# Second-layer S5 tables of a two-layer hybrid decoder: rotation tables as products of two tables of eight, GpSimd's products first, TensorE's parts later

## The chip, the cores and the metric

One core of a Trainium2 chip runs the whole program: two decoder layers over 512 tokens of width 1024, batch 1, in float32. The metric is the time of one execution on the device, in microseconds. The kernel before takes 1332.07 us in the median of 3 runs (1332.04 to 1332.51). TensorE is called PE in the rows of the profile, VectorE DVE, ScalarE ACT, GpSimd POOL; SP is the queue that issues the DMAs.

## What is computed

Each layer normalises x, projects it with `w_in`, sends parts of the result through three mixers (sparse attention, an S5 state-space group, a Mamba-2 group), projects back with `w_out` and adds; then it does the same with an MLP, `relu(h @ w_up)**2 @ w_down`. The change lies in the S5 group. What that group computes, cut to what matters:

```
step = exp(log_step); mag = exp(lr * step)
ab_re = mag * cos(li * step); ab_im = mag * sin(li * step)      # 16 groups x 64 complex states
bb_re, bb_im = ...                                              # input matrix, scaled by the step
x[s] = ab * x[s-1] + bb @ u[s]                                  # complex, along the 512 tokens
y[s] = Re(c @ x[s]) + d * u[s]
out  = gelu(y) * sigmoid(gelu(y) @ glu_w + glu_b)
```

All of `ab`, `bb` and `c` depend on the parameters alone, so the kernel makes tables of them which do not need the tokens.

## The kernel before, in words

**S5 in blocks of eight tokens.** The 512 tokens are 64 blocks (`C5`) of 8 (`T5`). Inside a block the recurrence is a matrix; from block to block the state is turned by the angle of `ab` to the power 8 and shrunk by `m8`, the magnitude to the power 8. The turning is taken out of the recurrence: VectorE multiplies by COS and SIN, scans with real factors, and turns back. `s5_tables` makes for each layer: the matrix `bb`; for each quarter `q` of the 16 groups the products `BPp` (bb times powers of ab, three GpSimd instructions) with `b0`, which TensorE transposes (tile `s5B`) and ScalarE copies to `BPT`; for each half the tables `COS` and `SIN`, 8 groups by 64 blocks; for each quarter the products `CA` (c times powers of ab), from which TensorE makes `s5st` (8 short matmuls in the trace for 4 in the code), ScalarE copies it to `strip`, GpSimd adds the term of `d`, and 8 DMAs on SP's queue spread it over the matrix `M` that GpSimd has cleared.

**COS and SIN before.** `s5_small` keeps cos and sin of the angle of one block times 1, 2, 4, ... 32 (`self.rot`, six pairs). A table starts with 1 and 0 in its first column and is doubled six times: columns k to 2k-1 are the first k turned by the angle of k blocks, with six instructions of 8k elements per half, 72 instructions in a layer.

**Who makes the order.** The program is written as streams (generators) that yield a length of time; `merge` always goes on with the stream whose clock is lowest. The instructions so written get ascending priorities, and a planner orders every engine's queue by priority and by when its own cost model takes each instruction to be ready. Engines run their queues in order. The first layer's tables are written beside its mixers (`mixers`). The second layer's are the stream `prepare`, written beside the first layer's MLP (`mlp`, 256 steps of 1.3 of the clock, 6 matmuls each); it starts at clock 120, and its GpSimd instructions are held behind the copy `gate` (L1395), which waits for the MLP's row statistics. While `prepare` runs, the pace of tables is that of the first layer, 0.3. A third stream, `stage`, splits the second layer's `w_in` and `w_out` into two parts and stores them in DRAM, through SP's queue as well. `rope_tables` of the second layer is written at the end of `prepare`.

**Buffers.** Tiles from `tt` share 16 buffers (tag "t"), tiles from `g` 52 (tag "g"). The scratch tiles `pt` have two buffers. A tile waits until an earlier tile's last reader has let its buffer go. In the kernel before the tables of one layer that live to the end are 4 BPT, 4 COS and SIN, 4 CA and 4 M, which is 16; bb, BPp and strip come from the same 16.

**Weights.** `Slabs` brings the weights through SP's queue (L176, or L167 for staged ones); ScalarE makes `whi` and VectorE `wlo` (L192) of each slab of the MLP. TensorE multiplies in three passes (L458 to L460).

Of the kernel before, what the change touches and what calls it, by code (L numbers as in the profile page):

```python
# [10 lines left out]
F32 = mybir.dt.float32  # L11
# [3 lines left out]
ALU = mybir.AluOpType  # L15
# [3 lines left out]
P = 128  # L19
# [15 lines left out]
G5 = 16  # L35
# [185 lines left out]
class Net:  # L221
# [271 lines left out]
    def s5_small(self):  # L493

        nc = self.nc
        v = nc.vector if S5_ON_DVE else nc.gpsimd
        n = L * G5
        o = _cc["lre"][0]
        lre = self.cols[:, o:o + n]
        o = _cc["lim"][0]  # L500
        lim = self.cols[:, o:o + n]
        o = _rr["lstep"][0]
        lst = self.rows[:, o:o + n]
        sg = self.tab_("sg")
        keep = lambda k: self.cp.tile([P, n], F32, name=f"s5{k}")
        tmp = self.small(n)
# [33 lines left out]
        ta = self.g([P, n, 4], name="s5ta")  # L540
# [21 lines left out]
        v.tensor_tensor(m8, m8, m8, ALU.mult)  # L562
        v.tensor_tensor(m8, m8, m8, ALU.mult)
        self.m8 = m8
        self.rot = []
        v.tensor_scalar(s1, s1, sg, None, ALU.mult)
        cc, ss = c1, s1
        for k in range(8):
            c2, s2 = (keep(f"rc{k}"), keep(f"rs{k}")) if k >= 2 else (tmp(), tmp())
            self.stt(v, s2, cc, 2.0, ss, ALU.mult, ALU.mult)  # L570
            v.tensor_tensor(t0, cc, cc, ALU.mult)
            v.tensor_tensor(t1, ss, ss, ALU.mult)
            v.tensor_tensor(c2, t0, t1, ALU.subtract)
            cc, ss = c2, s2
            if k >= 2:
                self.rot.append((cc, ss))
        yield 4.0

    def load_s5(self, l):
# [8 lines left out]
    def s5_tables(self, l, t):  # L588
# [38 lines left out]
            v.tensor_tensor(t, bu(u2), bw(w2), ALU.mult)  # L627
            v.tensor_tensor(out, out, t, ALU.add)

        for q in range(4):  # L630
            v = eng(f"B{q}")
            gs = slice(4 * q, 4 * q + 4)
            b0 = self.s([P, 4, 1, 16], tag=f"s5b0{q}", bufs=1)
            outer(v, b0, bbr, X, bbi, Y, gs, 0, 1)
            BPp = self.tt([P, 4, 16, 8], name="BPp")
            outer(v, BPp.rearrange("p g h d -> p g d h"), bbr, X, bbi, Y, gs, 1, 9)

            p = self.ps(self.bank["sB"], name="s5B")
            for j in range(4):
                nc.tensor.transpose(p[:, j * P:(j + 1) * P], BPp[:, j].rearrange("p h d -> p (h d)"), self.ident)  # L640
            bpt = self.tt([P, 4, P], name="BPT")
            nc.scalar.activation(bpt.rearrange("p g n -> p (g n)"), p, AF.Copy)
            t["b0"].append(b0)
            t["BPT"].append(bpt)
            yield self.pace["tab"] * 5.0

        for hf in range(2):
            v = eng(f"R{hf}")
            gs = slice(l * G5 + 8 * hf, l * G5 + 8 * hf + 8)
            cos = self.tt([P, 8, C5], name="COS")  # L650
            sin = self.tt([P, 8, C5], name="SIN")
            v.memset(cos[:, :, 0:1], 1.0)
            v.memset(sin[:, :, 0:1], 0.0)
            k = 1
            for j in range(6):
                ck, sk = [t[:, gs].unsqueeze(2).to_broadcast([P, 8, k]) for t in self.rot[j]]
                tmp = lambda: pt()[:, :8 * k].rearrange("p (g k) -> p g k", g=8)
                for out, op, f0, f1 in ((cos, ALU.subtract, ck, sk), (sin, ALU.add, sk, ck)):
                    ta, tb = tmp(), tmp()
                    v.tensor_tensor(ta, cos[:, :, :k], f0, ALU.mult)  # L660
                    v.tensor_tensor(tb, sin[:, :, :k], f1, ALU.mult)  # L661
                    v.tensor_tensor(out[:, :, k:2 * k], ta, tb, op)
                k *= 2
            t["COS"].append(cos)
            t["SIN"].append(sin)
            yield self.pace["tab"] * 13.0
        pool.tensor_scalar(bc[1], bc[1], self.tab_("sg"), None, ALU.mult)
        for q in range(4):
            v = eng(f"C{q}")
            gs = slice(4 * q, 4 * q + 4)  # L670
            ca = self.tt([P, 4, 8, 16], name="CA")
            outer(v, ca, cre, X, cim, Y, gs, 0, 8)
            p = self.ps(self.bank["sst"], (16, 4, 8, 16), name="s5st")
            for j in range(4):
                nc.tensor.matmul(p[:, j].rearrange("p d h -> p (d h)"), t["b0"][q][:, j, 0], ca[:, j].rearrange("p d h -> p (d h)"),
                                 start=True, stop=True)
            strip = self.tt([16, 4, 8, 16], name="strip")
            nc.scalar.activation(strip, p, AF.Copy)

            sh = [16, 4, 16]  # L680
            d = pt()[:16, :64].rearrange("p (g h) -> p g h", g=4)
            pool.tensor_tensor(d, self.ident[:16, :16].unsqueeze(1).to_broadcast(sh), dd[:, gs].unsqueeze(2).to_broadcast(sh), ALU.mult)
            pool.tensor_tensor(strip[:, :, 0], strip[:, :, 0], d, ALU.add)
            m = self.tt([P, 4, P], name="M5")
            pool.memset(m, 0.0)
            for i in range(8):
                nc.sync.dma_start(m[7 - i::8, :, i * 16:], strip[:, :, 0:8 - i].rearrange("p g d h -> p g (d h)"))
            t["CA"].append(ca)
            t["M"].append(m)
            yield self.pace["tab"] * 5.0  # L690


    def s5(self, l, tab, U, out):
# [888 lines left out]
```

## Time and profile before

| | |
|---|---|
| Median of 3 runs | 1332.07 us |
| Profiled execution | 1328.87 us |
| Its span | 1327.1 us |
| TensorE busy | 1218.0 us, 92% |
| VectorE busy | 885.2 us, 67% |
| ScalarE busy | 549.2 us, 41% |
| GpSimd busy | 169.7 us, 13% |
| Chain that ended last | TensorE 62%, VectorE 19%, issue 7%, GpSimd 6%, ScalarE 4% |

The span is the time between the first and the last instruction of the profiled execution; its own time includes what lies around. Busy shares are means over stages with different limits: the first layer's mixers lie between 0 and about 330 us, its MLP from there to about 700, the second layer's mixers up to about 960, and its MLP behind them.

### The profile page before, as it was taken

The page shows a single profiled execution, that of the slowest core. Times are in us where ns is not written, and L with a number is a line of the kernel's source. Part 1 is how long each engine was busy: PE and PEld are TensorE (multiplying, and loading weights), DVE is VectorE, ACT ScalarE, POOL GpSimd, SP SyncE. Part 2 cuts the span into 40 slices and gives each one's busy share as a digit, 9 for nine tenths or more (in the row PEclk, how much of TensorE's full clock was granted, in tenths as well). Part 3 has the DMA queues.
Part 4 walks back from the last instruction along what each step waited for, and adds up shares of the span by engine and source line. Part 5 has one row for each costly group of instructions (what it writes and reads, how often), then busy time and mean ns, then how long its engine had stood idle before and what let it go on. Part 6 is the DMA issues. An engine that isn't in the chain of part 4 may idle for free.

```text
span 1327.1 us, 17056 instructions
## 1 busy us (share of the span) xinstructions
PE 1218.0 (92%) x5708; PEld 977.1 (74%) x5708; DVE 885.2 (67%) x2024; ACT 549.2 (41%) x1128; POOL 169.7 (13%) x302
## 2 busy tenths in 40 slices
PE   5678957889999989999999989968999999999998
PEld 5566745458888868888888767754788888888887
DVE  5998999857886545665564699975475445444443
ACT  4245444664543533534443234455254233242331
POOL 2385100000796040000000000000000000000000
PEclk9889988899999999999999989978999999999999
DMA  5132220002567647677644634300323333333332
GB/s 189 40 88 70 74 74 24 9 1 72 148 213 257 214 146 252 224 262 230 227 149 137 219 120 124 120 17 1 111 88 97 101 97 96 96 96 99 100 110 81
DMA packets 139688, 161.64 MB, mean 122 GB/s; under 512 B 18768, under 2 KB 107600, under 8 KB 139600
## 3 DMA queue, kind: packets, MB, share of 16 engines
q1 hardware_dynamic: 139600, 160.55, 38.5%
q8 instruction: 45, 0.74, 0.2%
q14 instruction: 43, 0.35, 0.1%
HBM read 128.29 MB, written 31.03 MB: 120 GB/s over the span
## 4 chain that ended last, share of the span: by engine, by line
PE 62%; DVE 19%; issue 7%; POOL 6%; ACT 4%; DMA 1%; SPq 0%; ACTq 0%; DVEq 0%; POOLq 0%
PE pm L458 18%; PE pm L460 18%; PE pm L459 18%; PE po L1128 3%; DVE isc L1087 2%; DVE mx L1086 2%; DVE isc L1076 2%; PE pTp L1123 1%; DVE pe L1107 1%; DVE wlo L192 1%; DMA wraw<-in_w_in_dram 1%; POOL pt L660 1%; DVE cv L847 1%; ACT pe L1108 1%; POOL pt L661 1%
## 5 line engine op out<-in xcount | busy, mean ns | idle before, releaser
L192 DVE TENSOR_TENSOR wlo<-wraw,whi 128x512 fp32r<-128x512 f32 (+1 forms) x312 | 223.2, 718 | 243.0 <-ACT whi L191 241.4
L191 ACT ACTIVATE whi<-wraw 128x512 fp32r<-128x512 f32 (+1 forms) x312 | 194.1, 625 | 374.5 <-PE pm L459 236.9
L458 PE MATMUL pm<-xh,whi 128*128 128x512 f32 x640 | 252.4, 395 | 3.8 <-ACT q L1224 3.2
L460 PE MATMUL pm<-xh,wlo 128*128 128x512 f32 x640 | 250.1, 392 | 1.2 <-DVE wlo L192 1.2
L459 PE MATMUL pm<-xl,whi 128*128 128x512 f32 x640 | 250.9, 392 | 0.0
L460 PE MATMUL pm<-uh,wlo 128*128 128x512 f32 x512 | 199.7, 390 | 0.3 <-DVE wlo L192 0.3
L458 PE MATMUL pm<-uh,whi 128*128 128x512 f32 x512 | 199.6, 390 | 0.0
L459 PE MATMUL pm<-ul,whi 128*128 128x512 f32 x512 | 199.6, 390 | 0.0
L458 PEld LDWEIGHTS pm<-xh,whi 128*128 128x128 f32 x640 | 120.8, 189 | 30.8 <-ACT q L1224 3.9
L460 PEld LDWEIGHTS pm<-xh,wlo 128*128 128x128 f32 x640 | 120.6, 189 | 27.4 <-DVE wlo L192 2.0
L459 PEld LDWEIGHTS pm<-xl,whi 128*128 128x128 f32 x640 | 121.1, 189 | 24.2 <-issue 0.2
L460 PEld LDWEIGHTS pm<-uh,wlo 128*128 128x128 f32 x512 | 96.2, 188 | 20.8 <-DVE wlo L192 0.9
L459 PEld LDWEIGHTS pm<-ul,whi 128*128 128x128 f32 x512 | 96.3, 188 | 20.4 <-issue 0.4
L458 PEld LDWEIGHTS pm<-uh,whi 128*128 128x128 f32 x512 | 96.2, 188 | 20.3 <-issue 0.4
L458 PE MATMUL pm<-whi,xh 128*128 128x512 f32 (+1 forms) x176 | 67.4, 385 | 14.0 <-ACT xh L392 12.8
L460 PE MATMUL pm<-whi,xl 128*128 128x512 f32 (+1 forms) x176 | 66.6, 380 | 1.3 <-DVE xl L394 1.3
L459 PE MATMUL pm<-wlo,xh 128*128 128x512 f32 (+1 forms) x176 | 67.0, 381 | 0.5 <-DVE wlo L192 0.3
L1408 DVE TENSOR_TENSOR ul<-ur,uh 128x512 fp32r<-128x512 f32 x64 | 48.5, 758 | 21.0 <-ACT uh L1407 21.0
L1406 DVE SCALAR_TENSOR_TENSOR ur<-pm,ur 128x512 f32<-128x512 f32 x64 | 43.9, 686 | 23.0 <-ACT ur L1403 22.7
L1414 DVE TENSOR_TENSOR sq<-pm,r2b 128x512 f32<-128x512 f32 x64 | 44.1, 689 | 17.5 <-PE pm L460 17.5
L1407 ACT ACTIVATE uh<-ur 128x512 fp32r<-128x512 f32 x64 | 39.9, 624 | 30.7 <-DVE ur L1406 30.7
L1087 DVE MATCH_REPLACE8 isc<-mx,isc 128x256 f32<-128x256 f32 (+2 forms) x96 | 51.6, 541 | 0.0
(345 smaller groups left out, 1931.4 us busy)
## 6 DMA issues: line engine op xcount, KB each, us to landing
wraw<-in_w_up_dram SPq DMA_DIRECT2D x128, 256.0 KB, 2.8
wraw<-in_w_down_dram SPq DMA_DIRECT2D x128, 256.0 KB, 2.8
st<-shi SPq DMA_DIRECT2D x48, 256.0 KB, 2.9
st<-slo SPq DMA_DIRECT2D x48, 256.0 KB, 3.5
wlo<-st SPq DMA_DIRECT2D x48, 256.0 KB, 3.0
whi<-st SPq DMA_DIRECT2D x48, 256.0 KB, 2.8
wraw<-in_w_in_dram SPq DMA_DIRECT2D x32, 256.0 KB, 2.8
sraw<-in_w_in_dram SPq DMA_DIRECT2D x32, 256.0 KB, 3.9
```

Of the source, the lines that this page charges most:

```text
L191: nc.scalar.activation(hi, raw, AF.Copy)
L192: nc.vector.tensor_tensor(lo, raw, hi.bitcast(F32), ALU.subtract)
L458: nc.tensor.matmul(p, lh, rh, start=first, stop=False)
L459: nc.tensor.matmul(p, lh, rl, start=False, stop=False)
L460: nc.tensor.matmul(p, ll, rh, start=False, stop=last)
L1076: v.scalar_tensor_tensor(acc, r, wi[:, h:h + 1], acc, ALU.mult, ALU.add)
L1087: v.match_replace(acc, m8, acc, SENT)
L1128: nc.tensor.matmul(po[g_ * 64:g_ * 64 + 64], self.vt[:, kb, g_], pts[g_], start=kb == 0, stop=kb == b)
L1406: v.scalar_tensor_tensor(r, p, 0.0, r, ALU.max, ALU.mult)
L1407: nc.scalar.activation(h, r, AF.Copy)
L1408: v.tensor_tensor(lo, r, h.bitcast(F32), ALU.subtract)
L1414: v.tensor_tensor(t, d[1], rb, ALU.mult)
```

## The change

`rotc` and `rots` hold the six kept pairs as one tile each, so that the pairs for 1, 2, 4 and those for 8, 16, 32 blocks can be taken together (`j::3`). `c8` and `s8` are two tables of eight for all 16 groups: the angle of 0 to 7 blocks, and that of 0, 8, ... 56 blocks. They are made by three doublings of 32, 64 and 128 elements, 18 instructions in a layer. `COS` and `SIN` are then the products of the two: three instructions of 512 elements for each of them and each half, 12 in a layer.

`powers` and `turned`, and `taps` and `kernels`, are the two loops over `q`, each cut in two: GpSimd's products, and what follows them on TensorE, ScalarE, GpSimd (the term of `d`, clearing M) and SP. In the first layer the halves stand together as before. In the second the products are all written first, then 90 of the clock pass, then come the four `turned` and the four `kernels`, 6 of the clock apart. `strip` moves from the 16 buffers of "t" to the 52 of "g". The rotation step's pace goes from 13.0 to 7.0.

```diff
@@ s5_small
-        self.rot = []
+        self.rotc, self.rots = [self.cp.tile([P, 6, n], F32, name=self.nm("rot")) for _ in range(2)]
...
-            c2, s2 = (keep(f"rc{k}"), keep(f"rs{k}")) if k >= 2 else (tmp(), tmp())
+            c2, s2 = (self.rotc[:, k - 2], self.rots[:, k - 2]) if k >= 2 else (tmp(), tmp())
...
@@ s5_tables
-        for q in range(4):
+        def powers(q):
             v = eng(f"B{q}")
...
+            return b0, BPp
+        def turned(b0, BPp):
             p = self.ps(self.bank["sB"], name="s5B")
...
+        todo = []
+        for q in range(4):
+            todo.append(powers(q))
+            if l == 0:
+                turned(*todo[q])
             yield self.pace["tab"] * 5.0
+        v = eng("R0")
+        gs = slice(l * G5, (l + 1) * G5)
+        c8, s8 = [self.tt([P, 2, G5, 8], name=n) for n in ("c8", "s8")]
+        v.memset(c8[:, :, :, 0:1], 1.0)
+        v.memset(s8[:, :, :, 0:1], 0.0)
+        k = 1
+        for j in range(3):
+            ck, sk = [t[:, j::3, gs].unsqueeze(3).to_broadcast([P, 2, G5, k]) for t in (self.rotc, self.rots)]
+            tmp = lambda: pt()[:, :2 * G5 * k].rearrange("p (i g k) -> p i g k", i=2, g=G5)
+            for out, op, f0, f1 in ((c8, ALU.subtract, ck, sk), (s8, ALU.add, sk, ck)):
+                ta, tb = tmp(), tmp()
+                v.tensor_tensor(ta, c8[:, :, :, :k], f0, ALU.mult)
+                v.tensor_tensor(tb, s8[:, :, :, :k], f1, ALU.mult)
+                v.tensor_tensor(out[:, :, :, k:2 * k], ta, tb, op)
+            k *= 2
...
+            lo = [t[:, 0, 8 * hf:8 * hf + 8].unsqueeze(2).to_broadcast(sh8) for t in (c8, s8)]
+            hi = [t[:, 1, 8 * hf:8 * hf + 8].unsqueeze(3).to_broadcast(sh8) for t in (c8, s8)]
+            for out, op, x, y in ((cos, ALU.subtract, lo[0], lo[1]), (sin, ALU.add, lo[1], lo[0])):
+                o = out.rearrange("p g (a b) -> p g a b", a=8)
+                t8 = pt().rearrange("p (g a b) -> p g a b", g=8, a=8)
+                v.tensor_tensor(o, hi[0], x, ALU.mult)
+                v.tensor_tensor(t8, hi[1], y, ALU.mult)
+                v.tensor_tensor(o, o, t8, op)
...
-            yield self.pace["tab"] * 13.0
+            yield self.pace["tab"] * 7.0
...
-            strip = self.tt([16, 4, 8, 16], name="strip")
+            strip = self.g([16, 4, 8, 16], name="strip")
...
+        for q in range(4):
+            taps(q)
+            if l == 0:
+                kernels(q)
             yield self.pace["tab"] * 5.0
+        if l > 0:
+            yield 90.0
+            for q in range(4):
+                turned(*todo[q])
+                yield 6.0
+            for q in range(4):
+                kernels(q)
+                yield 6.0
```

## Rows read from the trace of the kernel before

**Rows 1.** Windows by stage: length, busy (count) per engine, TensorE clock, DMA.
```profile
76.00:99.00 23.00, 20.80 (x97) 15.96 (x95) 22.83 (x47) 13.27 (x27) 21.12 (x42) 0.93 0.33 92
...
115.00:170.00 55.00, 49.87 (x253) 38.31 (x252) 54.81 (x166) 27.75 (x63) 14.41 (x21) 1.00 0.28 75
300.00:455.00 155.00, 155.00 (x706) 128.94 (x705) 115.35 (x167) 69.19 (x122) 77.41 (x124) 1.00 0.58 179
455.00:500.00 45.00, 39.84 (x186) 31.34 (x185) 22.26 (x32) 16.80 (x30) 15.00 (x28) 0.96 0.52 157
500.00:700.00 200.00, 199.70 (x894) 165.25 (x892) 117.92 (x185) 84.72 (x147) 0.31 (x1) 1.00 0.69 224
770.00:840.00 70.00, 60.78 (x315) 48.98 (x314) 69.77 (x202) 27.13 (x58) 0.53 (x1) 0.93 0.41 127
...
490.00:495.00 5.00, 5.00 (x21) 3.70 (x19) 0.69 (x1) 1.22 (x2) 1.97 (x5) 0.76 0.19 29
```

**Rows 2.** TensorE's waits, whole span: total us, times, longest us.
```profile
PE s5st L675 <- POOL CA L628: 6.8, 3, 3.7
...
PE s5B L640 <- POOL BPp L628: 4.9, 1, 4.9
```

**Rows 3.** TensorE's timeline: start us, duration us, instruction, [idle before, releaser].
```profile
482.58 1.05 PE L675 MATMUL s5st<-CA,s5b 128*16 128x128 f32 x8 [1.42 <-POOL CA L628]
...
489.42 1.89 PE L675 MATMUL s5st<-CA,s5b 128*16 128x128 f32 x8 [3.75 <-POOL CA L628]
...
492.80 0.40 PE L460 MATMUL pm<-uh,wlo 128*128 128x512 f32 x1
...
504.72 1.05 PE L675 MATMUL s5st<-CA,s5b 128*16 128x128 f32 x8
...
506.73 0.39 PE L459 MATMUL pm<-ul,whi 128*128 128x512 f32 x1
...
510.82 0.50 PE L460 MATMUL pm<-uh,wlo 128*128 128x512 f32 x1 [0.30 <-DVE wlo L192]
```

**Rows 4.** GpSimd's timeline, from the gate to the second layer's last M.
```profile
340.80 0.56 POOL L1395 COPY gate<-r 128x4 f32<-128x4 f32 x1 [170.60 <-DVE r L1390]
...
377.86 0.65 POOL L660 TENSOR_TENSOR pt<-COS,s5rc 128x8 f32<-128x8 f32 x1
...
416.75 0.74 POOL L662 TENSOR_TENSOR SIN<-pt,pt 128x256 f32<-128x256 f32 x1
...
460.44 1.06 POOL L626 TENSOR_TENSOR CA<-s5bc,s5X 128x512 f32<-128x512 f32 x1 [37.93 <-PE s5B L640]
...
488.11 1.25 POOL L628 TENSOR_TENSOR CA<-CA,pt 128x512 f32<-128x512 f32 x1
...
794.38 0.53 POOL L685 MEMSET M<- 128x512 f32 x1 [287.55 <-PE s5v L709]
```

**Rows 5.** GpSimd's groups: operation, out<-in, count | busy us, mean ns | idle before.
```profile
L628 POOL TENSOR_TENSOR CA<-CA,pt 128x512 f32<-128x512 f32 x7 | 9.3, 1323 | 0.2
...
L626 POOL TENSOR_TENSOR CA<-s5bc,s5X 128x512 f32<-128x512 f32 x7 | 7.7, 1107 | 44.0 <-PE s5B L640 37.9 <-PE s5v L709 4.7 <-DMA M<-strip 1.4
...
L662 POOL TENSOR_TENSOR COS<-pt,pt 128x128 f32<-128x128 f32 x4 | 2.6, 642 | 0.3
```

**Rows 6.** VectorE's instruction ul (L1408) in two windows: length, busy (count), clock, DMA.
```profile
341.00:377.00 36.00, 8.56 (x6) 1.00 0.60 173
...
520.00:680.00 160.00, 11.01 (x16) 1.00 0.72 233
```

**Rows 7.** SP's queue, timeline: start us, duration us, line, DMA, count.
```profile
100.54 38.49 SPq L176 DMA_DIRECT2D wraw<-in_w_in_dram  x10
...
147.69 5.13 SPq L687 DMA_DIRECT2D M<-strip  x8
...
481.46 16.91 SPq L687 DMA_DIRECT2D M<-strip  x24
...
499.62 0.38 SPq L176 DMA_DIRECT2D wraw<-in_w_down_dram  x1
```

More of the change, by code (lines that the diff above doesn't have):

```diff
@@ L574, in s5_small @@
             cc, ss = c2, s2
-            if k >= 2:
-                self.rot.append((cc, ss))
         yield 4.0
@@ L647, in s5_tables @@
         for hf in range(2):
             v = eng(f"R{hf}")
-            gs = slice(l * G5 + 8 * hf, l * G5 + 8 * hf + 8)
             cos = self.tt([P, 8, C5], name="COS")
             sin = self.tt([P, 8, C5], name="SIN")
[L652 to L663, printed above, removed]
+            sh8 = [P, 8, 8, 8]
@@ L664, in s5_tables, with taps @@
             t["COS"].append(cos)
             t["SIN"].append(sin)
-            yield self.pace["tab"] * 13.0
+            yield self.pace["tab"] * 7.0
         pool.tensor_scalar(bc[1], bc[1], self.tab_("sg"), None, ALU.mult)
-        for q in range(4):
+        def taps(q):
             v = eng(f"C{q}")
@@ L672, in s5_tables, with kernels @@
             outer(v, ca, cre, X, cim, Y, gs, 0, 8)
+            t["CA"].append(ca)
+        def kernels(q):
+            gs = slice(4 * q, 4 * q + 4)
+            ca = t["CA"][q]
             p = self.ps(self.bank["sst"], (16, 4, 8, 16), name="s5st")
@@ L687, in s5_tables @@
                 nc.sync.dma_start(m[7 - i::8, :, i * 16:], strip[:, :, 0:8 - i].rearrange("p g d h -> p g (d h)"))
-            t["CA"].append(ca)
             t["M"].append(m)
+        for q in range(4):
+            taps(q)
+            if l == 0:
+                kernels(q)
             yield self.pace["tab"] * 5.0
+        if l > 0:
[6 more added lines that the diff above has]
+                yield 6.0
     def s5(self, l, tab, U, out):
```

## The prediction

> **What bounds the kernel now.** I read the page first (TensorE is busy for nine tenths of the span), then the windows by stage, then TensorE's waits, then the timelines of TensorE, GpSimd and the SP queue around the one hole that the windows show.
>
> The windows tell two kinds of stage apart [rows 1]. In the first layer's mixers VectorE is the full engine: 22.83 of 23 us from 76 to 99, 54.81 of 55 us from 115 to 170. In the first layer's MLP TensorE is: 155.00 of 155 us from 300 to 455, 199.70 of 200 us from 500 to 700. Between these lies the hole: from 455 to 500 TensorE is busy for 39.84 of 45 us. Here the second layer's tables are made beside the MLP. A microsecond that TensorE loses in an MLP is lost to the end, since nothing else is waited for there; a microsecond saved on GpSimd is worth only what somebody waits for it.
>
> TensorE's waits name the cause [rows 2]: its matmuls s5st wait for GpSimd's product CA, 6.8 us in three waits. Two are the hole, 1.42 us at 482.58 and 3.75 us at 489.42 [rows 3], together 5.17; the other 1.6 us lie in the first layer. In the hole's second half the granted clock is 0.76 [rows 1].
>
> GpSimd's timeline says why CA is late [rows 4]. The gate opens at 340.80; GpSimd makes BPp, turns the rotation tables from 377.86 to 417.49, begins CA, and then stands for 37.93 us until 460.44, waiting for TensorE's transposes s5B. The pool "t" has 16 buffers, and the next CA needs one that a BPp holds. TensorE reaches s5B only where the written order puts it, at the planner's clock 120. After it, three quarters of CA are still to be made while TensorE is due to use them a few microseconds later; the CA of 488.11 (1.25 us) ends at 489.36, and s5st starts at 489.42.
>
> **The change part by part.**
>
> *Second layer, order.* All GpSimd products are written at clock 120 to 136 and need 1 (bb) + 4 (BPp) + 2 (c8, s8) + 4 (COS, SIN) + 4 (CA) = 15 buffers of "t", which is within 16 since the strip moves to "g". So GpSimd no longer waits for TensorE. From the gate: BPp until some 377 as today, then the rotations, then CA. One CA takes two products of about 1.11 us and a sum of 1.32 us [rows 5], 3.5 us; four take 14.2 us. Everything is made by about 420. TensorE's parts follow at clock 120 + 4 x 1.5 + 2 x 2.1 + 4 x 1.5 + 90 = 226.2, the matmuls s5st from 250.2 to 268.2. A step of the MLP is 6 matmuls and 1.3 of the clock; 894 matmuls in 200 us [rows 1] make it 1.34 us, so a unit of the clock is 1.03 us. With clock 120 at 460, the transposes come at about 570 and s5st at 594 to 613, 150 us and more behind the last product. Both waits go:
> - idle time, 1.42 + 3.75 = 5.17 us [rows 3];
> - the slow clock behind the second: from the start of s5st to the fifth of the MLP's matmuls behind it, 492.80 - 489.42 = 3.38 us, against 506.73 - 504.72 = 2.01 us for the same piece at full clock [rows 3]: 1.37 us.
>
> Sum: 6.54 us, all on the path. The matmuls themselves, their evictions and the strips are the same in number and only move.
>
> *The moved steps on SP's queue.* Each of the four kernel steps issues 8 DMAs of M. Today 24 of them take SP 16.91 us without a break [rows 7], 0.70 us each, so 5.6 us for a step, now one every 6.2 us for 25 us, past which the weight loads must squeeze. Today SP brings no weights between 481.46 and 499.62, and TensorE loses 0.30 us to weights at 510.82 [rows 3]; but it stood for 5.17 us in that time. Bounds: -0.30 us (that wait goes) and +5.5 us (SP falls behind as far as today, and the 5.17 us of standing, in which TensorE used no weights, come on top of the 0.30). I take 0, nearest to the 0.30 of the row: loads now get in between four bursts.
>
> *Rotation tables.* 72 instructions of 8 to 256 elements per layer, 39.6 us in the second [rows 4], become 18 of 32 to 128 elements and 12 of 512. The long ones cost 1.11 to 1.32 us [rows 5], 13.3 to 15.8 us; the short ones at most 0.64 us (the 128-element row), 11.5 us at most. So 25 to 27 us at most, at least 12 us off GpSimd in each layer. In the second layer this lies in front of that lead and is worth nothing more. In the first, SIN and COS are read by VectorE long behind GpSimd's end, and VectorE is full; I take 0. Bounds: -1.6 us (the first layer's wait of s5st for CA [rows 2] goes) and +4.9 us (the largest wait of TensorE for a GpSimd product, s5B for BPp [rows 2], appears once more because the planner puts s5st earlier).
>
> *Long GpSimd instructions beside VectorE.* Where GpSimd ran 512-element instructions (341 to 377), VectorE's subtraction ul took 8.56 / 6 = 1.43 us; with GpSimd silent it took 11.01 / 16 = 0.69 us [rows 6]. The first layer's 12 long instructions will run at about 85 to 100, where VectorE is full. Between nothing and 12 x 0.74 = 8.9 us, I take 0: fewer GpSimd instructions in all stand against longer ones, the CA products that followed move to an earlier, less crowded stretch, and ul is one kind of instruction among many there. The Trainium skill, SBUF — State Buffer, section "Who interferes with whom", says that a VectorE instruction with two SBUF inputs and a GpSimd instruction that reads SBUF exclude one another for a whole instruction, whichever starts first. The rows on ul agree in kind; taken at its word for all twelve, it gives the third rival below.
>
> *The last M.* It no longer waits for a buffer until the second layer's s5v (794.38, after 287.55 us [rows 4]), and 8 DMAs leave SP's queue there. VectorE is full at that place, 69.77 of 70 us [rows 1], so 0; bounds 0 and -5.6 us (a whole burst off the path).
>
> **Sum.** The profiled execution took 1328.87 us (span 1327.1, 1.8 us around it). Less 6.5 this is 1322.4. The median of the runs, 1332.07, is 3.2 us above that execution; on its scale the forecast is 1332.07 - 6.5 = **1325.6 us**.
>
> **Rivals.**
> 1. *The moved DMAs crowd out the MLP's weights.* Four bursts, 90% of SP's time over 25 us, staging stores between them. For it: SP runs in order, and a burst that waits for its strip holds the loads behind it. Against: SP was closed for 18 us in one piece and TensorE lost 0.30. Price 5.5 us, the upper bound above: 1331.1 us.
> 2. *The other side: the first layer's M overtakes the projection weights.* Today SP ends its W_in loads at 139.03 and begins M at 147.69 [rows 7]. The rotations end at least 12 us sooner there, and with them CA, s5st and M may move up to about 135, in front of the last W_in loads, which then stand behind bursts of 5.6 us in a stage whose VectorE is full. Two bursts cost 11.3 us: 1325.6 + 11.3 = 1336.9 us. It decides from two bursts issued before the last W_in load. Against it: the first layer keeps its written order (every part of TensorE right behind its product), and M also waits for s5st in TensorE's own order, which a quicker GpSimd alone does not move.
> 3. *Long GpSimd instructions hold VectorE*, at full price, in the first layer: 1325.6 + 8.9 = 1334.5 us. For it: [rows 6]. Against: as above.
> 4. *The change doesn't do what it says*: TensorE still meets an unfinished product, because the planner takes the moved parts early. Against: BPp is done when the rotations start (377.86 [rows 4]), and TensorE takes s5B only before 460, in its written place. It would leave 1332.1 us.
>
> **How the numbers follow.** Forecast 0.60 (its own range 1321 to 1328.5), rival 1 0.10, rival 2 0.15, rival 3 0.10, rival 4 0.05. About 0.2% (2.7 us) is what a measurement of this kernel tells from no change: below 1329.4 is faster, above 1334.7 slower. Faster: 0.58 of the forecast and 0.02 of rival 1, whose price is a bound, 0.60. Slower: 0.13 of rival 2 and 0.04 of rival 3, 0.17. The rest, 0.23, is no change. The range from 1320.5 to 1335.0 leaves out about 0.05 below (the bounds of the first layer and of the last M both paid) and 0.14 above (most of rival 2).
>
> **What would show it.** TensorE's waits from 300 to 700 without s5st behind CA; TensorE busy without a hole until the MLP's end, granted clock 1.00 throughout; GpSimd's products in one piece from the gate to about 420, with no wait for s5B; s5B near 570 and s5st near 594 to 613; the memset of the last M before the second layer. The MLP of the first layer should be 6.5 us shorter, and the second layer as long as before. The forecast is wrong if TensorE waits for weights between 590 and 625 (rival 1), if the first layer's mixers are longer, with loads behind M on SP before 140 (rival 2) or VectorE's single instructions grow longer from 76 to 115 (rival 3), or if the second layer's length changes by more than 2 us.

## The result and the profile after

The kernel after took 1355.81 us, the median of four runs (1352.55 to 1357.84), against 1332.29 us before (1332.04 to 1332.91) on the same chip: a ratio of 1.0173, 95% interval 1.0155 to 1.0191. It is 1.7% slower. The forecast was 1325.6 us, with a range up to 1335.0: wrong in sign, and outside its range.

The profiled execution took 1357.66 us (span 1355.9; before 1327.1). Two marks divide the 28.8 us between the two spans: the gate, at which the first layer's MLP begins, and the last `rst` of VectorE, a few us into the second layer. The two executions lie further apart than the medians do (28.8 against 23.5 us): that of before ran 3.4 us below its median, that of after 1.9 us above. So the marks say where the time is lost; how much is better read from the medians.

| us | before | after | difference |
|---|---|---|---|
| first layer's mixers, start to gate | 340.80 | 368.71 | +27.9 |
| first layer's MLP, gate to last `rst` | 378.03 | 378.88 | +0.85 |
| second layer, to the end of the span | 608.3 | 608.3 | 0 |

Windows of after: length, busy time (count) of TensorE, weight load, VectorE, ScalarE, GpSimd; clock, DMA, GB/s. The first, third, fifth and last answer to [rows 1], the latter two moved by 28 us.

```profile
76.00:99.00 23.00, 15.97 (x72) 12.06 (x71) 22.93 (x36) 11.38 (x25) 22.12 (x31) 0.87 0.25 69
84.00:116.00 32.00, 15.65 (x69) 11.64 (x67) 31.73 (x31) 10.99 (x23) 28.67 (x31) 0.82 0.16 46
115.00:170.00 55.00, 51.08 (x244) 38.71 (x244) 46.98 (x137) 28.62 (x64) 4.50 (x7) 0.94 0.28 72
185.00:300.00 115.00, 81.71 (x407) 60.50 (x406) 94.58 (x255) 54.55 (x142) 0.00 (x0) 0.80 0.09 26
483.00:528.00 45.00, 45.00 (x200) 37.26 (x199) 29.08 (x47) 19.00 (x33) 0.00 (x0) 1.00 0.77 251
650.00:680.00 30.00, 24.21 (x99) 18.94 (x98) 13.93 (x21) 13.04 (x23) 3.81 (x13) 0.94 0.78 242
798.00:868.00 70.00, 60.55 (x315) 48.74 (x314) 69.81 (x203) 26.49 (x56) 0.00 (x0) 0.93 0.40 123
```

From 84 to 116 VectorE is busy throughout, with 31 instructions; before it did 49 in 26.73 us of that window. From 185 to 300, in the later part of the mixers, TensorE does 407 matmuls at a granted clock of 0.80, before 468 at 0.88. From 483 to 528 the hole of [rows 1] is closed: TensorE 45.00 of 45 us. A new one lies from 650 to 680. TensorE's waits of after from 345 to 745 are a single row, where [rows 2] had CA, and its timeline shows both pieces:

```profile
PE pm L458 <- ACT whi L191: 5.8, 2, 4.7
```
```profile
652.06 0.50 PE L458 MATMUL pm<-xh,whi 128*128 128x512 f32 x1 [1.12 <-ACT whi L191]
...
668.18 0.80 PE L458 MATMUL pm<-xh,whi 128*128 128x512 f32 x1 [4.66 <-ACT whi L191]
```

GpSimd's timeline of after (start, duration), against [rows 4]: from the gate to the last sum of CA (450.54) it does not wait for TensorE, and the four memsets of M stand well ahead of the second layer.

```profile
368.71 0.56 POOL L1433 COPY gate<-r 128x4 f32<-128x4 f32 x1 [196.33 <-DVE r L1428]
...
450.54 1.28 POOL L627 TENSOR_TENSOR CA<-CA,pt 128x512 f32<-128x512 f32 x1
...
598.49 0.53 POOL L710 MEMSET M<- 128x512 f32 x1 [145.97 <-PE s5B L642]
...
618.98 0.53 POOL L710 MEMSET M<- 128x512 f32 x1 [5.41 <-PE s5B L642]
```

SP's timeline of after (start, duration, count), against [rows 7]: in the first layer two bursts of M stand ahead of the last loads of `w_in`; in the MLP SP brings no weights between 625.81 and 648.23.

```profile
139.40 5.54 SPq L712 DMA_DIRECT2D M<-strip  x8
146.00 3.74 SPq L176 DMA_DIRECT2D wraw<-in_w_in_dram  x3
153.94 5.02 SPq L712 DMA_DIRECT2D M<-strip  x8
159.06 0.53 SPq L176 DMA_DIRECT2D wraw<-in_w_in_dram  x1
...
625.81 0.38 SPq L176 DMA_DIRECT2D wraw<-in_w_up_dram  x1
...
627.76 5.02 SPq L712 DMA_DIRECT2D M<-strip  x8
...
635.75 5.00 SPq L712 DMA_DIRECT2D M<-strip  x8
...
643.11 5.01 SPq L712 DMA_DIRECT2D M<-strip  x8
648.23 1.04 SPq L176 DMA_DIRECT2D wraw<-in_w_up_dram  x2
...
654.27 5.47 SPq L712 DMA_DIRECT2D M<-strip  x8
```

What VectorE does so long from 84 to 116 is read from two timelines of after side by side, VectorE's first, then GpSimd's.

```profile
93.39 1.08 DVE L1040 TENSOR_TENSOR rsw<-qi,cols 128x64 f32<-128x64 f32 x1
94.40 1.08 DVE L1033 TENSOR_TENSOR ksb<-ksb,rsw 128x48 f32<-128x48 f32 x1
95.41 1.33 DVE L1041 TENSOR_TENSOR rsw<-qi,cols 128x64 f32<-128x64 f32 x1
96.77 1.06 DVE L1042 TENSOR_TENSOR qi<-qi,cols 128x128 f32<-128x128 f32 x1
97.75 1.08 DVE L1040 TENSOR_TENSOR rsw<-qi,cols 128x64 f32<-128x64 f32 x1
```
```profile
93.21 1.18 POOL L681 TENSOR_TENSOR pt<-s,c 128x512 f32<-128x512 f32 x1
94.36 1.06 POOL L680 TENSOR_TENSOR COS<-c 128x512 f32<-128x512 f32 x1
95.38 1.27 POOL L682 TENSOR_TENSOR SIN<-SIN,pt 128x512 f32<-128x512 f32 x1
96.61 1.07 POOL L681 TENSOR_TENSOR pt<-s 128x512 f32<-128x512 f32 x1
97.64 1.11 POOL L680 TENSOR_TENSOR SIN<-c,s 128x512 f32<-128x512 f32 x1
```

GpSimd's groups of after from 60 to 130 (count, busy us, mean ns, idle before) price its long instructions as [rows 5] did the sums and products of CA, 1107 to 1323 ns:

```profile
L682 POOL TENSOR_TENSOR COS<-COS,pt 128x512 f32<-128x512 f32 x2 | 2.6, 1291 | 0.0
...
L681 POOL TENSOR_TENSOR pt<-s,c 128x512 f32<-128x512 f32 x2 | 2.3, 1145 | 0.0
```

The two engines run in step: one VectorE instruction to one GpSimd instruction, starts 0.03 to 0.18 us apart, whether VectorE has 48 elements to do or 128. The same instructions of before, beside GpSimd instructions of 64 and 128 elements (VectorE's timeline of before):

```profile
88.34 0.31 DVE L1002 TENSOR_TENSOR rsw<-qi,cols 128x64 f32<-128x64 f32 x1
88.58 0.20 DVE L995 TENSOR_TENSOR ksb<-ksb,rsw 128x48 f32<-128x48 f32 x1
88.69 0.36 DVE L1003 TENSOR_TENSOR rsw<-qi,cols 128x64 f32<-128x64 f32 x1
89.09 0.51 DVE L1004 TENSOR_TENSOR qi<-qi,cols 128x128 f32<-128x128 f32 x1
```

A handy mark for this loss is VectorE's first `hhl`, behind that stretch: 99.49 before, 115.74 after, 16.25 us later. A second part, 27.9 - 16.25 = 11.7 us, is lost between it and the gate. By these two executions there were three things to explain: 16 us by 116, 12 us from there to the gate, and an MLP that gained nothing.

### The profile page after: what moved, and what is told of

Read it like the earlier page. It is cut to its first block, busy times and chain, and to the rows that moved or that the text cites. A ratio compares the mean times of both kernels' runs of the same rounds, so it can differ in the third digit from the quotient of the medians.

```text
span 1355.9 us, 16979 instructions
## 1 busy us (share of the span) xinstructions
PE 1228.9 (91%) x5708; PEld 986.7 (73%) x5708; DVE 911.5 (67%) x2024; ACT 549.9 (41%) x1128; POOL 157.0 (12%) x214
## 4 chain that ended last, share of the span: by engine, by line
PE 68%; DVE 10%; ACT 4%; issue 2%; SPq 1%; DMA 0%; POOL 0%; ACTq 0%; DVEq 0%; POOLq 0%
PE pm L458 20%; PE pm L459 20%; PE pm L460 20%; PE po L1166 2%; DVE isc L1125 2%; PE pTp L1161 2%; DVE mx L1124 2%; ACT pe L1146 1%; DVE isc L1114 1%; DVE pe L1145 1%; PE hTp L1084 1%; PE lg L1093 1%; DVE cv L885 1%; PE bct L428 0%; PE ssdy L945 0%
## 5 line engine op out<-in xcount | busy, mean ns | idle before, releaser
L192 DVE TENSOR_TENSOR wlo<-wraw,whi 128x512 fp32r<-128x512 f32 (+1 forms) x312 | 236.8, 762 | 230.4 <-ACT whi L191 224.2
L458 PE MATMUL pm<-whi,xh 128*128 128x512 f32 (+1 forms) x176 | 68.4, 390 | 13.7 <-ACT xh L392 12.6
L1446 DVE TENSOR_TENSOR ul<-ur,uh 128x512 fp32r<-128x512 f32 x64 | 45.2, 706 | 20.6 <-ACT uh L1445 20.4
L1478 DVE TENSOR_TENSOR slo<-sraw,shi 128x512 fp32r<-128x512 f32 (+1 forms) x56 | 45.0, 804 | 12.2 <-ACT shi L1477 12.2
```

Of the source, the lines that this page charges most:

```text
L192: nc.vector.tensor_tensor(lo, raw, hi.bitcast(F32), ALU.subtract)
L458: nc.tensor.matmul(p, lh, rh, start=first, stop=False)
L1446: v.tensor_tensor(lo, r, h.bitcast(F32), ALU.subtract)
L1478: nc.vector.tensor_tensor(lo, raw, hi.bitcast(F32), ALU.subtract)
```

## The experiments

Each kernel was compared with the kernel before on the same chip (medians of before: 1330.91 for the first four, 1332.49 for the next four, then 1331.54 and 1331.23). The marks are from its one profiled execution, and kernels with the same first layer scatter: the three with that of e1 have the gate from 341.73 to 343.57, the two with that of after at 363.76 and 368.71. So beside a difference of gates the text gives that of the times, taken from the ratios (0.0010 is 1.3 us); an interval reaches 1 to 3 us to either side.

| kernel | time, ratio with 95% interval | `hhl` | gate | MLP |
|---|---|---|---|---|
| before | | 99.49 | 340.80 | 378.03 |
| after | 1355.81, 1.0173 (1.0155 to 1.0191) | 115.74 | 368.71 | 378.88 |
| e1 old rotations in the first layer | 1331.09, 1.0001 (0.9992 to 1.0010) | 100.29 | 342.18 | 377.69 |
| e2 pace 13 | 1350.62, 1.0147 (1.0132 to 1.0163) | 116.25 | 362.04 | 377.45 |
| e3 products cut in four | 1343.60, 1.0098 (1.0078 to 1.0118) | 100.41 | 354.48 | 377.37 |
| e4 M steps spaced | 1347.47, 1.0130 (1.0113 to 1.0147) | 115.93 | 363.76 | 370.71 |
| e5 order only | 1344.27, 1.0094 (1.0079 to 1.0109) | 100.20 | 358.45 | 377.79 |
| e6 as e1, M steps spaced | 1323.24, 0.9936 (0.9923 to 0.9949) | 100.64 | 341.73 | 370.71 |
| e7 cut, old order, spaced | 1325.95, 0.9955 (0.9943 to 0.9967) | 100.57 | 343.89 | 370.72 |
| e8 as e1, M on GpSimd's queue | 1324.44, 0.9932 (0.9908 to 0.9956) | 99.62 | 343.57 | 370.74 |
| e9 cut, pace 11 | 1341.40, 1.0089 (1.0064 to 1.0115) | 100.37 | 351.71 | 379.24 |
| e10 cut, pace 12 | 1343.41, 1.0090 (1.0075 to 1.0105) | 100.22 | 354.90 | 376.51 |
| e11 long instructions only | 1340.38, 1.0069 (1.0051 to 1.0088) | 113.21 | 353.85 | 377.63 |
| e12 as e5, first M on GpSimd's queue | 1338.40, 1.0054 (1.0037 to 1.0071) | 101.07 | 350.28 | 376.93 |
| e13 as after, first M on GpSimd's queue | 1346.88, 1.0118 (1.0103 to 1.0133) | 115.93 | 358.91 | 377.46 |

**e1: where the loss is.** The first layer's rotation block is put back.

```diff
+        if l == 0:
+            for hf in range(2):
...
+                for j in range(6):
...
+                yield self.pace["tab"] * 13.0
+        else:
+            v = eng("R0")
...
-            strip = self.g([16, 4, 8, 16], name="strip")
+            strip = (self.tt if l == 0 else self.g)([16, 4, 8, 16], name="strip")
```

> The kernel after, but the first layer makes its rotation tables as before (72 short GpSimd instructions, pace 13, strip among the 16 buffers); the second layer stays as changed. If the whole loss before the gate (340.80 before, 368.71 after, 27.9 us) comes from the first layer's rotation tables, the gate returns to about 341 and the time falls from 1355.8 to about 1328 to 1333: 1333 if the first layer's MLP keeps its +0.8 us (6.5 us won, 7.3 us lost again to weights), 1326 if that loss belonged to the late start and goes too. Rival: the second layer's order or something else in the program's end slows the first layer through the shared planner; then the gate stays above 360 and the time above 1350.

The time is that of before, 1.0001. All that was lost is lost in the first layer's mixers, and the reordering of the second layer's tables, alone, is worth nothing as it stands: the MLP keeps 377.69 us.

**e2: the pace alone.**

```diff
-            yield self.pace["tab"] * 7.0
+            yield self.pace["tab"] * (13.0 if l == 0 else 7.0)
```

> The kernel after with one number changed: in the first layer the step behind each pair of rotation tables is given 13.0 on the writing clock again, not 7.0. GpSimd runs the same instructions, with all twelve of 512 elements; the order of the other engines in the first layer's mixers is nearly that of before (the head of block 3 of the index scores is in its old place). Theory, two causes: the long GpSimd instructions hold VectorE (about 17 us by 115) and the changed order costs some 10 us more by 290; then the gate comes at about 358 and the time is 1344 to 1348. Rival A, contention alone (the late VectorE is all, the order does nothing): gate at 368, time 1355. Rival B, the order alone: gate at 341, time about 1333, and VectorE's short instructions between 84 and 100 take 0.2 to 0.5 us again.

Between the forecasts: 1350.62, with the gate at 362.04. By the gates the old pace brings back 2 to 7 us of 23 to 28, by the times 3.5 of 23; VectorE's short instructions are as long as in after (`hhl` at 116.25). So what the pace alone does to the order is a small part of the loss. The order of this kernel was not quite that of before (the strip's buffers differ); e11 mends that.

**e3: the length of one GpSimd instruction.**

```diff
-                v.tensor_tensor(o, hi[0], x, ALU.mult)
-                v.tensor_tensor(t8, hi[1], y, ALU.mult)
-                v.tensor_tensor(o, o, t8, op)
+                for c0 in range(0, 8, 2) if l == 0 else (0,):
+                    gg = slice(c0, c0 + 2) if l == 0 else slice(0, 8)
+                    v.tensor_tensor(o[:, gg], hi[0][:, gg], x[:, gg], ALU.mult)
+                    v.tensor_tensor(t8[:, gg], hi[1][:, gg], y[:, gg], ALU.mult)
+                    v.tensor_tensor(o[:, gg], o[:, gg], t8[:, gg], op)
```

> The kernel after, but in the first layer each of the twelve products of 512 elements is cut into four of 128 elements, so 48 instead of 12; the order of VectorE, ScalarE and SP is the same as after. GpSimd's work does not shrink: 48 times 0.42 to 0.66 us (rows of 128 elements) is 20 to 32 us against 14.5 us. Theory, a VectorE instruction of two inputs waits until the running GpSimd instruction ends: its rotations of 64 elements, now 1.08 to 1.36 us, should take 0.5 to 0.7 us, the loss of 16 us by 115 falls to 6 to 10 us and the time to 1344 to 1350. Rival, VectorE loses by what GpSimd moves in all, whatever the length of one instruction: the same rows stay at 1.1 us or the loss grows, 1356 to 1362.

VectorE's order is the same as in after, and GpSimd has four times as many of these products and no less work. `hhl` returns from 115.74 to 100.41: of 16.25 us only 0.9 are left, better than forecast; the time, 1343.60, lies 0.4 us below its forecast. VectorE's timeline of e3, the instructions shown above for after:

```profile
89.64 0.48 DVE L1042 TENSOR_TENSOR rsw<-qi,cols 128x64 f32<-128x64 f32 x1
90.05 0.48 DVE L1035 TENSOR_TENSOR ksb<-ksb,rsw 128x48 f32<-128x48 f32 x1
90.45 0.46 DVE L1043 TENSOR_TENSOR rsw<-qi,cols 128x64 f32<-128x64 f32 x1
90.94 0.40 DVE L1044 TENSOR_TENSOR qi<-qi,cols 128x128 f32<-128x128 f32 x1
```

They take 0.40 to 0.48 us beside GpSimd instructions of 0.40 to 0.57, still in step. What VectorE pays is the length of the other engine's single instruction, not what that engine moves in all. But the gate is at 354.48 still, 13.7 us later than before, and the time is 13.0 us longer, in a kernel in which VectorE is on time at `hhl`. That must come from the order, which is that of after.

**e4: room between the bursts.**

```diff
-            yield 90.0
+            yield 20.0
...
                 kernels(q)
-                yield 6.0
+                yield 24.0
```

> The kernel after, but in the second layer's tables the pause before TensorE's parts is 20 instead of 90 and the four steps that issue the DMAs of M lie 24 apart instead of 6, so 8 DMAs (5.0 us of SP) in each 24 us rather than 32 in 32 us; the first layer is untouched. Theory, the four bursts close together keep the weight loads off SP (none between 625.81 and 648.23) and TensorE then waits 5.8 us for weights and runs slow for a while: those waits go, and the time falls by about 7 us, to 1349. Rival, the loss in that stage has another cause (the clock, the stage's own DMAs): the time stays at 1355 to 1357 and a wait for whi of 4 to 5 us is still there.

1347.47, as forecast: the MLP falls from 378.88 to 370.71 us, and no wait for `whi` is left. The reordering is worth 378.03 - 370.71 = 7.3 us in the MLP, and in after the four close bursts take back 8.2 us, more than all of it (5.7 us by the times of after and e4).

**e5: the order without the long instructions.** As e1, but with the pace and the strip of after; GpSimd's instructions in the first layer are those of before.

```diff
-                yield self.pace["tab"] * 13.0
+                yield self.pace["tab"] * 7.0
...
-            strip = (self.tt if l == 0 else self.g)([16, 4, 8, 16], name="strip")
+            strip = self.g([16, 4, 8, 16], name="strip")
```

> The kernel after, but the first layer makes its rotation tables by the 72 short instructions of before, with the new pace 7.0 behind each half. So GpSimd's instructions there are those of before, while TensorE and ScalarE take their work in the first layer's mixers in exactly the order of the run with the products cut in four (gate at 354.48), and VectorE's differs from it in 4 places. Theory, the pace alone moves one head of the index scores and what follows it, and that costs 12 to 13 us: gate at 352 to 356, time 1342 to 1345. Rival, those 13 us came from the cut products themselves or from c8 and s8: the gate is back at 341 to 343 and the time at 1331.

Time as forecast, gate (358.45) slightly beyond. By the gates the order alone costs 17.7 us here and 13.7 in e3, by the times 12.5 and 13.0, so the two agree. One number for how soon the tables are written, and a strip's pool, are worth that much with not one instruction changed. The forecast put it on the pace alone, but e5 differs from e1 in both; e11 takes them apart.

**e6 and e8: the second layer's gain by two ways.** Both have the first layer of e1. e6 has the spacing of e4 (the same four lines); e8 keeps the steps 6 apart and changes the queue:

```diff
-                nc.sync.dma_start(m[7 - i::8, :, i * 16:], strip[:, :, 0:8 - i].rearrange("p g d h -> p g (d h)"))
+                (nc.sync if l == 0 else nc.gpsimd).dma_start(m[7 - i::8, :, i * 16:], strip[:, :, 0:8 - i].rearrange("p g d h -> p g (d h)"))
```

> The first layer as before, the second layer's tables with all GpSimd products first, pause 20 and the four M steps 24 apart. Theory: the reordering is worth the 6.5 us that TensorE loses in the hole of before, and only the four bursts took them back (4.4 us of waits for weights plus slow clock in the same kernel with steps 6 apart, 1331.1 us); spaced they cost nothing, so the MLP is 6 to 7 us shorter than before and the time is 1324 to 1326. Rival: the bursts hurt wherever they stand, because TensorE now runs through and needs every weight load in time: a wait for whi of 1 us or more remains and the time is 1328 to 1331.

> The first layer as before, the second as after with the M steps still 6 apart, but their 32 DMAs issued from GpSimd's queue and not from SP's: the same bytes at about the same time. Theory, SP's time to issue them (0.62 us each) keeps the weight loads waiting: TensorE's waits for whi (4.4 us in the kernel that issues them from SP) go and the time is 1324 to 1327. Rival, the transfers of M themselves (4-byte-wide rows scattered over partitions) slow the weights' transfers: the waits stay at 3 us or more and the time at 1330 to 1332.

1323.24 and 1324.44: both beat the kernel before, by 0.64% and 0.68%, and both have the same MLP, 370.71 and 370.74 us. (e6's time lies 0.8 us below its forecast. The aside on 4-byte rows in e8's text is wrong: a run of M is 16 to 128 elements of 4 bytes.) In e8 the same DMAs are issued at the same places, 4.05 to 4.24 us for eight on GpSimd, and TensorE waits for no weights in the MLP; so it was SP's time to issue them, not their traffic. SP's timeline of e6: a burst every 26 to 27 us with loads between.

```profile
527.34 5.03 SPq L734 DMA_DIRECT2D M<-strip  x8
...
538.13 1.35 SPq L176 DMA_DIRECT2D wraw<-in_w_up_dram  x2
540.52 0.43 SPq L176 DMA_DIRECT2D wraw<-in_w_up_dram  x1
542.89 4.30 SPq L176 DMA_DIRECT2D wraw<-in_w_down_dram  x3
...
554.45 5.01 SPq L734 DMA_DIRECT2D M<-strip  x8
```

**e7: tables of eight without either loss.** The cut of e3, the spacing of e4, and in the first layer pace and strip of before:

```diff
-            yield self.pace["tab"] * 7.0
+            yield self.pace["tab"] * (13.0 if l == 0 else 7.0)
...
-            strip = self.g([16, 4, 8, 16], name="strip")
+            strip = (self.tt if l == 0 else self.g)([16, 4, 8, 16], name="strip")
```

> Tables of eight in both layers, with the first layer's products cut into four of 128 elements, the pace 13.0 and the strip of before there, so that TensorE's order in the first layer is that of before; the M steps of the second layer spaced 24 apart. Theory, length of the GpSimd instructions and the pace are the whole loss of the first layer: gate at 341 to 344, time 1324 to 1328, as with the old rotations. Rival, the tables of eight cost something of their own beside VectorE (they start the products of CA earlier): gate at 346 or more, time 1330 or more.

1325.95, as forecast (gate 343.89). With short instructions and the old order the tables of eight are about as good as the old ones, and no better: the ratio is 2.5 us above that of e6, and the two intervals just overlap.

**e9 and e10: is it one head of the index scores?** The trace of after shows the last head of block 3's index scores at 219.56 on TensorE, 160.91 before, and the selection that needs it ends 35 us later (last MAX8 262.40 before, 297.74 after). The planner puts the head back in front at pace 12, not at 11. Both kernels have the products cut as in e3; e10 has 12.0 in the place of 11.0.

```diff
-            yield self.pace["tab"] * 7.0
+            yield self.pace["tab"] * (11.0 if l == 0 else 7.0)
```

> The kernel with the products cut in four, the pace of the first layer's rotation step at 11.0. In the order of TensorE the last head of block 3's index scores still stands behind the GLU's matmuls, as with pace 7.0. Theory, the place of this one head is what costs 12 to 17 us before the gate: gate at 352 to 358, time 1342 to 1346. Rival, the loss falls with the pace by and by (many small moves of the order): from 354.5 at pace 7 to some 342 at pace 13, so about 346 at pace 11, time 1335 to 1337.

> The same with pace 12.0. Here the planner puts the last head of block 3's index scores in front of the S5 matmuls s5v again, as before the change; elsewhere the order differs from before in many places. Theory, the place of the head decides: gate at 341 to 345, time 1330 to 1334. Rival, many small moves: 343 to 346, time 1333 to 1336, hardly less than with pace 11; only the two runs together tell them apart, a jump of 9 us or more against a step of 2 to 3 us.

The theory fell. With the head early (e10: last MAX8 at 241.47, sooner than before) the gate is at 354.90, not sooner than with it late (e9: 351.71). Nor does the loss shrink by and by: the gate is at 354.48, 351.71 and 354.90 for pace 7, 11 and 12 (13.0, 11.9 and 12.0 us by the times), and at 343.89 in e7, whose order is that of before. What the losing orders have in common is the S5 input `u`, computed by VectorE at 157.2 to 158.3 in before, e1, e6, e7 and e8, and at 164.0 to 165.6 in e3, e5, e9 and e10. The bursts of M are not what they share: in e10 the last load of `w_in` ends at 142.81 and M begins behind it, at 148.79.

**e11: the long instructions without the order.** As e2, with the strip of before in the first layer; TensorE's order there is exactly that of before.

```diff
-            strip = self.g([16, 4, 8, 16], name="strip")
+            strip = (self.tt if l == 0 else self.g)([16, 4, 8, 16], name="strip")
```

> The kernel after with pace 13.0 and the strip of the first layer among the 16 buffers, so that TensorE's order in the first layer's mixers is exactly that of before while GpSimd still runs the twelve products of 512 elements. Theory, the long instructions cost the 16 to 17 us by which VectorE is late at 116 and nothing behind that: gate at 357 to 359, time 1346 to 1349. Rival, being late there costs more later (slow clock, attention starting late): gate at 361 to 363, time 1350 to 1353.

Gate 353.85 and 1340.38 us: lower than both forecasts. VectorE is 13.7 us late at `hhl` and 13.05 us at the gate (12.9 and 11.7 us against e1, whose VectorE order is the same), and the program takes 9.2 us longer (interval 6.8 to 11.7). So no more is lost behind `hhl`; that part of the theory holds. The size was too large in part because it was taken from after, where one more instruction (`wlo`, 4.37 us at 105.18) was held through several GpSimd instructions. Against e2 the strip's pool alone moves the gate by 362.04 - 353.85 = 8.2 us and the time by 10.4 us (at `hhl` it is 3.0 us, since `wlo` is held in e2 as in after). So the pool has a large part in what the order costs. With short instructions and the strip among the 52 buffers, 12 to 13 us are lost at pace 7, 11 and 12 alike (e3, e9, e10). No run has the short pace with the old pool, so the pace's own share is not shown.

**e12 and e13: M on SP ahead of `w_in`.** The queue of the first layer's M is changed, in e5 and in after.

```diff
-                nc.sync.dma_start(m[7 - i::8, :, i * 16:], strip[:, :, 0:8 - i].rearrange("p g d h -> p g (d h)"))
+                (nc.gpsimd if l == 0 else nc.sync).dma_start(m[7 - i::8, :, i * 16:], strip[:, :, 0:8 - i].rearrange("p g d h -> p g (d h)"))
```

SP's timeline of e5, the kernel to be mended in e12; before, the loads of `w_in` end at 139.03 [rows 7]:

```profile
126.77 5.59 SPq L734 DMA_DIRECT2D M<-strip  x8
133.36 5.70 SPq L176 DMA_DIRECT2D wraw<-in_w_in_dram  x3
143.31 5.02 SPq L734 DMA_DIRECT2D M<-strip  x8
148.43 0.53 SPq L176 DMA_DIRECT2D wraw<-in_w_in_dram  x1
```

> The run with the old rotations and pace 7.0 (gate at 358.45), but the 32 DMAs of M in the first layer are issued from GpSimd's queue. In that run two bursts of M stand on SP at 126.77 and 143.31, ahead of the last W_in loads (133.36 to 148.96; they end at 139.03 before the change), as the second rival of the prediction had it. TensorE's order is the same but for one instruction. Theory, these bursts hold up the W_in loads and with them the projections and u: the last W_in load is issued by 140, gate at 344 to 348, time 1331 to 1335. Rival, the order of the engines themselves costs it and SP's order has no part: gate at 354 to 359, time 1342 to 1346.

> The kernel after with the 32 DMAs of M in the first layer issued from GpSimd's queue and nothing else changed. On SP two bursts (139.40 and 153.94) stand ahead of the last W_in loads there too. Theory, bursts ahead of W_in cost part of the loss: gate falls from 364 to 369 (two profiles of the same first layer) to about 356 to 358 (the long instructions alone cost 13, run with pace 13.0 and the old strip), time 1344 to 1347. Rival, SP's order has no part in it: gate stays at 362 or more, time 1351 or more.

A part of it. The gate falls by 8.2 us in e12 (358.45 to 350.28) and by 4.9 to 9.8 us in e13 (to 358.91); by the times it is 5.3 and 7.3 us. The time of e13 is as forecast, its gate just beyond; e12 misses both. And the gain does not come by way of the `w_in` loads. SP's timeline of e12 has the loads in one row, and the last ends at 147.46:

```profile
86.49 60.97 SPq L176 DMA_DIRECT2D wraw<-in_w_in_dram  x16
```

That is 1.5 us sooner than in e5 (148.96); in e13 it is 156.62 against 159.59 in after. `u` comes at 164.90 in e12, hardly sooner than in e5 (165.3). VectorE's order changed along with the queue (in 36 places before the gate, in both kernels), so what gave the 5.3 to 7.3 us is open. In e12 a gate 9.5 us late remains, 7.2 us by the time: the order of the engines itself. Which of its many small moves delays `u` was not settled.

## Why the prediction was wrong

**Second layer, order (-6.54 us): right.** The waits for CA are gone and GpSimd works in one piece. Less the 27.9 us by which the gate is late, its last product ends at 423.9 (forecast: about 420), s5B starts at 569.9 (570) and the four s5st start between 597.8 and 620.4 (594 to 613). The MLP of e4 and e6 to e8, 370.71 to 370.74 us, is 7.3 us shorter for it.

**The moved DMAs (taken as 0, at most +5.5): the first step that failed.** They took 8.2 us in after, and e1's MLP, 377.69 us, shows 7.0 by the same reckoning. I reasoned that SP's bursts had cost 0.30 us before. But that was read where TensorE stood for 5.17 us and used no weights; with the standing gone, the reserve of weights runs out. SP also brought none for longer, 22.4 us against 18, and no run tells the two apart. Of the 8.2 us, 5.8 are waits, and the clock of 0.94 over the 30 us from 650 to 680 would make another 1.8 (an estimate). I had this as rival 1, with the right mechanism and too low a price, and gave it 0.10. "Loads now get in between four bursts" was wrong: none came between the first three, since the staging stores and bursts stood one behind the other. (A burst takes SP 5.0 us in before too; the 5.6 of the prediction shares out 16.91 us that are not without a break, since SP waited 1.6 us for a strip in them.)

**Rotation tables (0) and rival 2: failed.** GpSimd did become free sooner, but in the first layer nothing waited for that, and two bursts of M moved ahead of the last `w_in` loads, the sign that rival 2 had named. Its mechanism is not borne out: with M off SP 5.3 to 7.3 us come back (price 11.3), but the last `w_in` load ends only 1.5 to 3.0 us sooner (e12, e13), and e10 loses as much with M behind it. The step that I did not have at all is the planner's answer: a shorter pace and another pool for the strip together gave the first layer a different order, which costs 12.5 to 13.0 us of time (e5, e3) and 7.2 us even with M off SP (e12); the pool alone moves the time by 10.4 us (e2 against e11). I had written that the first layer "keeps its written order"; it keeps it only within the tables' own stream.

**Long GpSimd instructions beside VectorE (0, at most 8.9): failed.** They cost 12.9 us at `hhl` (e11 against e1) and 9.2 us of time (e11 against before). The mechanism was named as rival 3; what failed is the choice of 0, and in the price the count. In e11 and e1 VectorE takes the same instructions in the same order. At `ksb` (88.04 in e11, 86.76 in e1) e11 is 1.28 us behind, and 19 instructions later, at `wlo` (VectorE's timelines of e11, then of e1), 14.43 us:

```profile
109.77 0.68 DVE L192 TENSOR_TENSOR wlo<-wraw,whi 128x512 fp32r<-128x512 f32 x1
```
```profile
95.34 1.22 DVE L192 TENSOR_TENSOR wlo<-wraw,whi 128x512 fp32r<-128x512 f32 x1
```

That is 0.69 us for each, near the 0.74 read from `ul` [rows 6]; but 19 instructions of VectorE were held there, not 12. Behind `hhl` a part of this is made good, and that 12 x 0.74 = 8.9 comes near what is left of it in the time is luck. Nor is 0.74 a steady price; the same two windows of after, 28 us later (length, busy and count of `ul` alone, clock, DMA, GB/s), give 5.01 / 6 = 0.84 us and 10.57 / 16 = 0.66 us, a difference of 0.18:

```profile
369.00:405.00 36.00, 5.01 (x6) 1.00 0.67 195
548.00:708.00 160.00, 10.57 (x16) 0.99 0.67 213
```

The first layer's stretch is full of instructions that take 0.2 to 0.5 us, and nearly each of these was stretched to 1.04 to 1.36 us, the length of GpSimd's. And GpSimd's long ones were more than twelve: the products and sums of CA moved forward into the same stretch behind them. "Fewer GpSimd instructions in all stand against longer ones" had the sign wrong: fewer and longer is just what leaves VectorE fewer turns. The Trainium skill, SBUF — State Buffer, section "SBUF: two separate sides", says that whoever comes first (a VectorE instruction with two SBUF inputs, or a GpSimd instruction that reads SBUF) holds the shared ports for its whole instruction, the other being blocked and not slowed. After and e3 agree (1.06 to 1.33 us beside instructions of 1.06 to 1.27 us, 0.40 to 0.48 beside 0.40 to 0.57), and the rule taken at its word for every VectorE instruction in the stretch would have warned of it.

**The last M (0): right**; the second layer is as long as before, 608.3 us.

**The sum of the parts.** By the times, long instructions 9.2 (e11) and order 12.5 to 13.0 (e5, e3) make 21.7 to 22.2 us, against 22.9 for both together (after less e1): within the intervals they add up. The gates, each of one execution, give 13.0 and 13.7 to 17.7 against 23.0 to 27.9, which is too rough to show that one part hides behind another. I had set rivals 1, 2 and 3 beside each other as alternatives of 0.35 in all. They were not alternatives: 1 and 3 both happened, and the sign of 2. Their prices added to the forecast, 1325.6 + 5.5 + 11.3 + 8.9, give 1351.3 us, near the measured 1355.8, but by luck: the 11.3 of rival 2 stands where an order that I had not priced costs 12.5 to 13.0.

## What to carry to other kernels

- Where VectorE is full, a GpSimd instruction beside it costs by its length, once for each VectorE instruction that it holds: make such instructions as short as VectorE's own, or run them where VectorE has room; twelve long for 72 short ones was a bad exchange (e3, e11).
- When a stall is taken away, price the other queues as if the engine had never stood: bursts that were free behind the stall may now be late (e1 against e6), and rivals with different places add up.
- With a planner, compare the engines' order before and after wherever a pace or a buffer pool is touched; here that alone was worth 12.5 to 13.0 us (e5, e3), and the pool of one small tile alone 10.4 us (e2 against e11).
- A mark of one profiled execution says where time goes, not how much: the gates of the same first layer lay up to 5 us apart, and put the long instructions at 13.0 us where the times say 9.2.

## What the runs showed of the hardware that was not expected

VectorE and GpSimd take turns even when VectorE's part is tiny: an instruction of 128x24 elements took 1.04 us at 90.96 in after, the one behind it (128x24 as well) 0.17 us at 91.92. In these rows the price is the wait for a foreign instruction or nothing, not a share.

One VectorE instruction can be held for several turns: `wlo`, 0.68 us at 99.83 in before, took 4.37 us at 105.18 in after, while GpSimd started five instructions of 0.52 to 1.28 us.

Issued from GpSimd's queue, eight DMAs of M took that queue 4.05 to 4.24 us (e8), against 5.0 to 5.5 us on SP's (after).

The granted clock of the stretch in which TensorE is not full differs between two runs of the same first layer: 0.80 from 185 to 300 in after, 0.86 in e4, with 4.95 us between their gates.
